# Output projection of a hybrid decoder layer: weight splits in contiguous columns, a strided stationary operand, other last copies and another step order

## The chip, the cores and the metric

One core of a Trainium2 chip runs the whole layer. The metric is the device time of one execution in microseconds (us), as the median of several runs. Five engines work side by side, each with its own instruction list, in order: TensorE (PE; PEld is its weight loading), VectorE (DVE), ScalarE (ACT), GpSimd (POOL) and SyncE (SP), which here issues nearly all transfers. An instruction waits on semaphores that other engines or transfers raise.

## The reference

One decoder layer over 256 tokens of width 1024, all in fp32. What matters here is the end of the token mixer and the beginning of the mixture of experts:

```python
merged = jax.nn.sigmoid(gate_a) * (o_attn @ w_branch_attn[l]) + jax.nn.sigmoid(gate_r) * (o_rwkv @ w_branch_rwkv[l])
h = h + gt1 * (merged @ w_out[l])
xn2 = _rmsnorm(h, moe_norm_g[l]) * (1.0 + sc2) + sh2
moe = _hier_moe(xn2.reshape(B * S, D), ...)
h = h + gt2 * moe.reshape(B, S, D)
```

Before it stand a sparse attention branch (8 heads, with an indexer that selects 64 keys for each query) and an RWKV-7 branch (8 heads, a recurrent state). The experts are 32 SwiGLU MLPs of 1024 x 512; every token uses two of them, and the weights of all 32 are read, 201 MB in all.

## The kernel before, in words

The program has three stretches.

*The mixing stage.* Five generators (rwkv, selection, attention, gate, modulation) yield after each piece of TensorE work, and a loop takes their steps in the order that the string `ORDER` writes out by hand, one letter for a step. `LORD` is the order in which the weights of this stage are loaded. `pump()` issues loads into a large SBUF arena as long as there is room; `RESERVE[stage]` is the room that it leaves free in each stage. All loads go through SyncE's queue, in order, and a load waits until the buffer that it fills has been let go.

*Split matmuls.* [...] `split()` (lines 510 to 521) makes of a weight tile of 512 columns a high part (a copy that rounds to fp32r, by ScalarE, line 519, or GpSimd, line 517) and a low part (weight less high part, line 520, by VectorE or GpSimd). `SPLIT[stage]` says which engines do it, with two letters for each of four splits in turn: "AP" is a copy on ScalarE and a subtraction on GpSimd. `mm3()` (lines 528 to 532) does three matmuls: high x high, high x low, low x high. Split tiles lie in a ring of four pairs of 512 columns.

*The output projection* (lines 1493 to 1514). The merged branches, transposed to channels x tokens, lie in `mh` and `ml` (high and low), 8 blocks of 128 channels. `w_out` comes in four loads of two k each (k is a block of 128 of the 1024 input channels). The 1024 output channels are dealt out to 8 blocks m with a stride of eight: block m holds the channels m, m + 8, m + 16 and so on. Before the change the split reads the weights with that stride, so that the split tile holds four blocks of 128 neighbouring columns, and one split serves four blocks (12 matmuls). In the last round (j = 3) four splits are made and the blocks are finished one by one: residual and gate (line 1506), squares for the norm (lines 1509 to 1513), router logits (line 1471). Then come the routing on VectorE (lines 1549 to 1599), the transposes of h (line 1483) and the first matmuls of the experts.

*The experts.* Quadruples of experts: gather, gate and up projections (lines 1611, 1626, 1632), down projections (line 1653, in the last quadruple 1660 and 1666), merge by a matmul (line 1708). Their weights flow through the arena; a buffer is let go when its matmuls are done, and then SyncE loads the next. At the end `leave()` (lines 1784 to 1793) copies the sums from PSUM, for the second half of the tokens in two parts of 256 columns, and sends them out.

Other lines that are named later: 406 (modulation), 1063 (transposes of x, whose columns are taken eight apart), 1086 and 1101 (selection scores), 360 (a step of a reciprocal root on VectorE), 798 (scores of the rwkv branch), 1172 (transposes of normalised heads), 1323 and 1325 (merging and splitting the branches' sum).

Of the kernel before, what the change touches and what calls it, by code (L numbers as in the profile page):

```python
# [45 lines left out]
INV = 18.0  # L46
SOFT = 4.5
TMAJ = 0.3
NP2 = 4
NPO = 4  # L50
REST = 12.0
SMALL = 2432
WRS = True
MODS = ((0, 0, 0), (1, 0, 0, 1), (1, 0, 0, 1), (1, 0, 0, 0))
ALIGN = 1024
RESERVE = (29696, 12288, 15360, 4096, 0)
FORCE = False
FORCE0 = True
WIDE = 'a'
_S = ("AD", "PD", "AP", "PD")  # L60
SPLIT = (('PD', 'PD', 'AP', 'AD'), ('PD', 'PD', 'AP', 'PD'), ('PP', 'PP', 'AD', 'AD'), ('AD', 'AP', 'AD', 'AD'), ('AD', 'PD', 'AP', 'PD'))
PRIO = ('mod', 'sel', 'rwkv', 'attn', 'gate')
ORDER = 'rrrrrrmrrmmrrmrrmrrrrrrmrrrmmmrrmrmmmmrsrmaarmrmarrramrmamrrmraarrmmaarmarmaasrmmasaasmmsrarssrasraaarrarrarraasrssasssararasgrssssgraargrsrgsrsgggsrrsmgmmgsmrrrrggrgrgrrggggrsaggrrrggrgrrrgagagaggggaaaagggggaaaggaagggagagggaggaaaaagaggaaaaaggaaaaaaaggaggggggggggg'
LORD = (0, 1, 2, 3, 4, 5, 6, 7, 8, 9, 10, 12, 13, 15, 11, 14, 17, 16, 18, 23, 19, 20, 21, 22, 24, 28, 25, 27, 26, 29, 30, 31, 32, 33, 34, 35, 36, 37, 38, 44, 40, 39, 41, 42, 51, 45, 43, 47, 48, 52, 50, 46, 49)
INFO = []
QUADS = NE // 4
ENDS = ((0, 512), (512, 512))
# [90 lines left out]
def layer_kernel(tc, I, out, dbg=None):  # L158
    nc = tc.nc
    dbg = dbg or (lambda name, ap: None)  # L160
    ALL = CFG[2]
    TOT = ALL - 6144 - 1024 * NP2
    RING = CFG[0] * 4096
    ctxs = []

# [8 lines left out]
    NB = {"r": 3, "a": 3, "g": 2, "e": 4}  # L174
    A = Arena(sb.tile([128, TOT], F32, name="arena"), TOT)

    nB2 = 2048 + 1024 * (NP2 - NPO)
    nB = ALL - TOT - nB2
    fr = tc.tile_pool(name="fr", bufs=1)
    B = Arena(fr.__enter__().tile([128, nB], F32R, name="split"), nB)  # L180
    fr2 = tc.tile_pool(name="fr2", bufs=1, side="right")
    B2 = Arena(fr2.__enter__().tile([128, nB2], F32R, name="split2"), nB2)
    state = {"t": 0.0, "dma": 3.0, "next": 0, "stage": 0, "tag": "a", "more": []}

    def MM(lo, hi, shape, dtype=None):
        ap = A.get(*shape, lo=lo, hi=hi, dtype=dtype)
        assert ap is not None, ("arena full", shape)
        return ap

    def M(*shape, dtype=None):  # L190
        small = np.prod(shape) < 300
        ap = A.get(*shape, lo=TOT - SMALL, hi=TOT, dtype=dtype) if small else None
        return MM(RING, TOT if small else TOT - SMALL, shape, dtype) if ap is None else ap

# [12 lines left out]
    def add_ada(r, js):  # L207
        for j in js:
            add_load(("ada", r, j), (1, 2048), [(None, ada[:, j:j + 1, 2048 * r:2048 * r + 2048])])
# [41 lines left out]
    for i, l in enumerate(base):  # L251
        loads.append(l)
        for key in ad[ADAL[i - 14][0]:ADAL[i - 14][1]] if 0 <= i - 14 < len(ADAL) else ():
            add_ada(key[1], (key[2],))
    if LORD:
        loads[:] = [loads[i] for i in LORD]
    INFO.append(len(loads))
# [6 lines left out]
    for q in range(QUADS):  # L264
        for n, name, r in (("eg", "expert_w_gate", 4), ("eu", "expert_w_up", 4), ("ed", "expert_w_down", 2)):
            for i, (c, m) in enumerate(ENDS if n == "ed" and q == QUADS - 1 else ((0, None), (0, None))):
                for e in range(4 * q, 4 * q + 4 if q or n != "eg" or i else 0):
                    w = I[name][0, e].rearrange("(p k) n -> p k n", p=128)
# [7 lines left out]
    def pump():  # L276
        while state["next"] < len(loads):
            key, shape, parts = loads[state["next"]]
            t = A.get(*shape, lo=0, hi=RING, from_top=False)
            if t is None and A.room(RING, TOT - SMALL) >= int(np.prod(shape)) + (RESERVE[state["stage"]] if state["next"] >= nst else 6144):  # L280
                t = A.get(*shape, lo=RING, hi=TOT if state["stage"] == 4 else TOT - SMALL)
            for m in state["more"] if t is None else ():
# [10 lines left out]
    def need(key):  # L293
        assert key in W, ("not loaded", key, list(W))
        return W[key]

    def done(key, then=None):
        t = W.pop(key)
        next(a for a in [A] + state["more"] if id(t) in a.live).free(t)
        if then is not None:  # L300
            then()
        pump()
# [195 lines left out]
    def step(it, keep):  # L498

        return after_last(lambda: next(it, "end"), keep)  # L500
# [4 lines left out]


    cnt_split = [0]
    pairs = [(b.get(512), b.get(512)) for b in [B] * NPO + [B2] * (NP2 - NPO)]

    def split(w, p=None):  # L510

        i = cnt_split[0]
        cnt_split[0] += 1
        h, l = (t.rearrange("p (k n) -> p k n", k=w.shape[1]) for t in pairs[i % len(pairs)])
        p = p or SPLIT[state["stage"]][i % 4]
        if p[0] == "P":
            nc.gpsimd.tensor_scalar(h, w, 1.0, 0.0, op0=OP.mult, op1=OP.add)  # L517
        else:
            nc.scalar.copy(h, w)  # L519
        (nc.gpsimd if p[1] == "P" else nc.vector).tensor_sub(l, w, h.bitcast(F32))  # L520
        return h, l
# [6 lines left out]
    def mm3(ps, l, r, start, stop):  # L528

        nc.tensor.matmul(ps, l[0], r[0], start=start, stop=False)  # L530
        nc.tensor.matmul(ps, l[0], r[1], start=False, stop=False)  # L531
        nc.tensor.matmul(ps, l[1], r[0], start=False, stop=stop)  # L532
# [794 lines left out]
    mh, ml = xhi, xlo  # L1327
# [91 lines left out]
    while todo:  # L1419

        at = {n: max(ready[n], came[blocked[n]] + 0.5) if blocked[n] else ready[n] for n in todo
              if blocked[n] is None or blocked[n] in W}
        want = [n for n in at if nth < len(ORDER) and n[0] == ORDER[nth]]
        if want:
            at = {n: at[n] for n in want}
        t = max(state["t"], min(at.values()))
# [12 lines left out]
        c = step(it, FORCE)  # L1439
# [12 lines left out]
            blocked[n] = c  # L1452
    row2, sh2, s2c, rb, gt1 = (res[n] for n in ("row2", "sh2", "s2c", "rb", "gt1"))
    state["stage"] = 4
    del pairs[NPO:]
    fr2.__exit__(None, None, None)
    state["more"].append(Arena(pool(name="sb1", bufs=1, side="right").tile([128, nB2], F32, name="more0"), nB2))
    A.free(*[c[0] for c in cur.values() if c[0] is not state["nwt"]])
# [9 lines left out]
    def logits(m):  # L1468

        for a in range(2):  # L1470
            nc.tensor.matmul(psl[:, 64 * a:64 * a + 36], h[:, m, 128 * a:128 * a + 128], wrt[:, m, :],  # L1471
                             start=False, stop=False)
# [13 lines left out]
    def block(m):  # L1486
        return pso[m // 2][:, 256 * (m % 2):256 * (m % 2) + 256] if m < 6 else pso[m - 3][:, 0:256]

    def out_part(m, k, w, i):
        mm3(block(m), (w[0][:, i, :], w[1][:, i, :]), (mh[:, k, :], ml[:, k, :]), k == 0 and m > 5,  # L1490
            k == 7 and m not in (0, 2, 4))

    for j in range(4):
        w = need(("wo", j))
        ws = {}
        for hh, kk in ((0, 0), (0, 1), (1, 0), (1, 1)) if j == 3 else ((0, 0), (1, 0), (0, 1), (1, 1)):
            ws[hh, kk] = split(w[:, kk, :].rearrange("p (c k) -> p k c", k=8)[:, 4 * hh:4 * hh + 4, :])
            for i in range(4 if j < 3 else 0):
                out_part(4 * hh + i, 2 * j + kk, ws[hh, kk], i)
            for m in range(4 * hh, 4 * hh + 4 if j == 3 and kk else 0):  # L1500
                for k2 in range(2):
                    out_part(m, 6 + k2, ws[hh, k2], m % 4)
                for n in {3: (0,), 4: (1,), 5: (2,), 6: (3,), 7: (4, 5)}.get(m, ()):
                    logits(n)
                for n in () if m in (0, 2, 4) else (m - 1, m) if m < 6 else (m,):
                    nc.vector.scalar_tensor_tensor(h[:, n, :], block(n), gt1[:, n:n + 1], h[:, n, :], op0=OP.mult, op1=OP.add)
                    sq = hsq[:, 0 if n == 0 else 1 + (n + 1) % 2, :]
                    if n == 7:
                        nc.vector.tensor_mul(sq, h[:, n, :], h[:, n, :])
                    else:  # L1510
                        nc.scalar.activation(sq, h[:, n, :], AF.Square)
                    if 0 < n < 6:
                        nc.gpsimd.tensor_add(hsq[:, 0, :], hsq[:, 0, :], sq)
        done(("wo", j))
# [15 lines left out]
    def ME(*shape, dtype=None):  # L1530
        return next(ap for ap in (a.get(*shape, dtype=dtype) for a in [A] + state["more"]) if ap is not None)
# [144 lines left out]
    acc = [acp.tile([128, 512], F32, name=f"acc{i}") for i in range(4)]  # L1676
# [33 lines left out]
    y = None  # L1710
# [63 lines left out]
    y = ME(2, D)  # L1774
# [9 lines left out]
    def leave(c):  # L1784

        for a in range(2):
            o = acc[2 * a + c // 512]
            if a == 0:
                nc.scalar.copy(y[:, a, c:c + 512], o)
            else:  # L1790
                nc.vector.tensor_copy(y[:, a, c:c + 256], o[:, 0:256])
                nc.scalar.copy(y[:, a, c + 256:c + 512], o[:, 256:512])
            (nc.scalar if a else nc.sync).dma_start(out=out[0, 128 * a:128 * a + 128, c:c + 512], in_=y[:, a, c:c + 512])

    last[0] = None
# [2 lines left out]
    times_gate(0, ps)  # L1798
    after_last(lambda: finish(st, 0, stop=True))
    leave(0)  # L1800
    ps, p4 = PS(), PS()
    after_last(lambda: cols_down(ps, [need(("ed", e, 1)) for e in es[0:3]]))
# [3 lines left out]
    after_last(lambda: finish(st, 512, 96))  # L1806
    after_last(lambda: finish(sl, 512, 128, 0, True))
    leave(512)
    for i in range(2):
        for e in es:  # L1810
# [142 lines left out]
```

## Time and profile before

| | us |
|---|---|
| three runs | 797.19, 797.26, 798.94 |
| median | 797.26 |
| profiled execution | 798.72 |
| its span, first to last instruction | 796.8 |
| TensorE matmuls busy | 676.4 |
| VectorE, ScalarE, GpSimd busy | 285.3, 167.6, 144.2 |
| granted TensorE clock, mean (1 is full) | 0.948 |
| moved by DMA | 261.38 MB, mean 328 GB/s |

The profiled execution lies 1.46 us above the median. Its time holds 1.9 us more than the span. Busy shares are averages over stages of different kinds: in the mixing stage all four compute engines work, in the experts only TensorE and the DMA engines do much. A row of the timeline gives start, duration, engine, line, operation and shapes, and in brackets how long the engine had been idle before and what ended that.

### The profile page before, as it was taken

What the parts mean: (1) busy time and instruction counts of PE and PEld (TensorE: products, weight loads), DVE (VectorE), ACT (ScalarE), POOL (GpSimd) and SP (SyncE); (2) the same over time, 40 slices, a digit from 0 to 9 for tenths busy, and PEclk for the clock granted to TensorE, in tenths of its full rate; (3) what the DMA queues carried; (4) which work ended last, traced back from release to release, by engine and by line L of the source; (5) the groups of instructions that cost most, each with busy time, mean ns of one, the idle gap of its engine ahead of it and who ended that gap; (6) DMA issues with size and microseconds to landing.
All of it is one profiled execution on the core that took longest, in us unless ns stands there. A gap on an engine that the chain in (4) does not pass through costs nothing.

```text
span 796.8 us, 11470 instructions
## 1 busy us (share of the span) xinstructions
PE 676.4 (85%) x4657; PEld 364.7 (46%) x4657; DVE 285.3 (36%) x665; ACT 167.6 (21%) x347; POOL 144.2 (18%) x176
## 2 busy tenths in 40 slices
PE   5897989799998998889999778878768868878667
PEld 2785657468888877853342312312312312312112
DVE  2577789697336557741210160100100100100001
ACT  2445412144156644321110100100100100000000
POOL 1446744331314117610000000000000000000000
PEclk9899999899999999989999899899999999899889
DMA  9997467443656456779999999999999999999994
GB/s 333 389 308 253 165 221 282 146 154 105 218 208 239 133 178 246 292 257 420 422 421 422 421 420 422 421 420 423 420 421 422 420 421 422 420 421 422 422 392 180
DMA packets 63590, 261.38 MB, mean 328 GB/s; under 512 B 7952, under 2 KB 19216, under 8 KB 38448
## 3 DMA queue, kind: packets, MB, share of 16 engines
q1 hardware_dynamic: 63248, 260.11, 83.4%
q8 instruction: 37, 0.61, 0.3%
q10 hardware_dynamic: 288, 0.52, 0.2%
q14 instruction: 17, 0.14, 0.0%
HBM read 259.57 MB, written 1.05 MB: 327 GB/s over the span
## 4 chain that ended last, share of the span: by engine, by line
DMA 46%; PE 10%; DVE 3%; SPq 1%; issue 1%; POOL 1%; ACT 0%; POOLq 0%; DVEq 0%
DMA arena<-in_expert_w_down_dram 17%; DMA arena<-in_expert_w_gate_dram 13%; DMA arena<-in_expert_w_up_dram 12%; DMA more<-in_expert_w_gate_dram 2%; DMA more<-in_expert_w_up_dram 2%; PE ps_e L1626 2%; DVE split L520 1%; PE ps_e L1611 1%; SPq L288 1%; PE ps_e L1660 1%; PE acc L1701 1%; PE acc L1708 1%; PE ps_e L1653 1%; PE ps_e L1632 0%; PE ps_r L1471 0%
## 5 line engine op out<-in xcount | busy, mean ns | idle before, releaser
L1626 PE MATMUL ps_e<-arena,more 128*32 128x512 f32 x440 | 87.6, 656 | 23.9 <-DMA arena<-in_expert_w_gate_dram 12.0
L1626 PE MATMUL ps_e<-arena 128*32 128x512 f32 x416 | 82.4, 682 | 20.4 <-DMA arena<-in_expert_w_gate_dram 11.7
L1653 PE MATMUL ps_e<-arena 128*32 128x512 f32 x360 | 84.3, 609 | 13.5 <-DMA arena<-in_expert_w_down_dram 9.6
L520 DVE TENSOR_TENSOR split<-arena,split 128x512 fp32r<-128x512 f32 x77 | 70.7, 928 | 45.6 <-ACT split L519 31.8
L1637 ACT ACTIVATE arena<-ps_e 128x512 f32<-128x512 f32 x8 | 4.8, 597 | 244.8 <-PE ps_e L1626 244.8
L1638 DVE SCALAR_TENSOR_TENSOR arena<-arena,ps_e 128x512 f32<-128x512 f32 x8 | 5.5, 688 | 140.2 <-ACT arena L1637 140.2
L1691 POOL TENSOR_TENSOR arena<-arena 128x256 f32<-128x256 f32 x8 | 4.9, 615 | 280.7 <-PE ps_e L1694 279.0
L1670 DVE TENSOR_TENSOR arena<-ps_e,more 128x512 f32<-128x512 f32 (+1 forms) x17 | 11.8, 691 | 122.2 <-PE ps_e L1653 109.1
L519 ACT CAST split<-arena 128x512 fp32r<-128x512 f32 x66 | 45.0, 688 | 48.1 <-PE ps_g L531 30.3
L520 POOL TENSOR_TENSOR split<-arena,split 128x512 fp32r<-128x512 f32 x33 | 47.2, 1431 | 42.6 <-ACT split L519 27.8
L564 PE MATMUL ps_a<-split 128*128 128x256 f32 x360 | 52.1, 304 | 3.1 <-ACT split L476 1.9
L1626 PEld LDWEIGHTS ps_e<-arena,more 128*32 128x32 f32 x440 | 19.4, 118 | 76.3 <-issue 30.9
L564 PEld LDWEIGHTS ps_a<-split 128*128 128x128 f32 x360 | 47.9, 205 | 12.1 <-issue 6.5
L1626 PEld LDWEIGHTS ps_e<-arena 128*32 128x32 f32 x416 | 17.8, 122 | 74.0 <-issue 35.8
L517 POOL TENSOR_SCALAR split<-arena 128x512 fp32r<-128x512 f32 x44 | 36.9, 842 | 70.2 <-PE ps_g L531 18.7
L1653 PEld LDWEIGHTS ps_e<-arena 128*32 128x32 f32 x360 | 19.6, 110 | 64.3 <-issue 31.2
L530 PE MATMUL ps_g<-split 128*128 128x256 f32 x128 | 39.1, 306 | 0.0
L532 PE MATMUL ps_g<-split 128*128 128x256 f32 x128 | 36.9, 289 | 2.0 <-POOL split L520 2.0
L1639 DVE SCALAR_TENSOR_TENSOR arena<-arena,ps_e 128x512 f32<-128x512 f32 x8 | 8.2, 1029 | 82.5 <-PE ps_e L1626 82.5
L531 PE MATMUL ps_g<-split 128*128 128x256 f32 x128 | 36.8, 288 | 0.0
L1611 PEld LDWEIGHTS ps_e<-arena,more 128*128 128x128 f32 x256 | 30.7, 195 | 13.2 <-issue 8.2
L532 PE MATMUL ps_a<-split 128*128 128x256 f32 (+1 forms) x96 | 30.4, 317 | 6.2 <-DVE split L520 6.2
(378 smaller groups left out, 1192.5 us busy)
## 6 DMA issues: line engine op xcount, KB each, us to landing
arena<-in_expert_w_gate_dram SPq DMA_DIRECT2D x54, 1024.0 KB, 19.8
arena<-in_expert_w_up_dram SPq DMA_DIRECT2D x53, 1024.0 KB, 19.8
arena<-in_expert_w_down_dram SPq DMA_DIRECT2D x53, 1024.0 KB, 19.8
arena<-in_w_in_dram SPq DMA_DIRECT2D x18, 1024.0 KB, 7.8
arena<-in_ada_w_dram SPq DMA_DIRECT2D x16, 1024.0 KB, 6.1
more<-in_expert_w_up_dram SPq DMA_DIRECT2D x11, 1024.0 KB, 19.8
more<-in_expert_w_down_dram SPq DMA_DIRECT2D x11, 1024.0 KB, 19.8
arena<-in_ada_w_dram SPq DMA_DIRECT2D x16, 512.0 KB, 10.9
```

Source lines behind the costliest of these rows:

```text
L517: nc.gpsimd.tensor_scalar(h, w, 1.0, 0.0, op0=OP.mult, op1=OP.add)
L519: nc.scalar.copy(h, w)
L520: (nc.gpsimd if p[1] == "P" else nc.vector).tensor_sub(l, w, h.bitcast(F32))
L530: nc.tensor.matmul(ps, l[0], r[0], start=start, stop=False)
L531: nc.tensor.matmul(ps, l[0], r[1], start=False, stop=False)
L532: nc.tensor.matmul(ps, l[1], r[0], start=False, stop=stop)
L564: nc.tensor.matmul(p, a[:, kk, :], b[:, 4 * hf + kk, :], start=(i == 0 and kk == KORD[0]), stop=(i == 2 and kk == KORD[-1]))
L1611: nc.tensor.matmul(ps[:, n * kk:n * kk + n], h2[:, a, 2 * k2 + kk, :], oh(a), start=(a == 0), stop=(a == 1))
L1626: nc.tensor.matmul(ps[32 * g:32 * g + 32, :], xg[:, 4 * i + k, 32 * g:32 * g + 32], w[:, k, :], start=(i == 0 and k == 0), stop=(i == 1 an ...
L1639: nc.vector.scalar_tensor_tensor(hidb[0:r].rearrange("p (j q) -> p q j", j=4), thb[0:r].rearrange("p (q j) -> p q j", j=4), 0.5, psu[0:r, ...
L1653: nc.tensor.matmul(pss[c][32 * g:32 * g + 32, :], hTb[:, 2 * i + j, 32 * g:32 * g + 32], w[:, j, 512 * c:512 * c + 512], start=(i == 0 and ...
L1670: nc.vector.tensor_mul(Yb[0:r, c:c + 512], ps[0:r], gt2[0][0:r, g:g + 512])
```

## The change

Four things are done.

1. In the output projection the weights are split as they lie, in two halves of 512 neighbouring columns for each k. The four ring pairs are now two wide pairs of 1024 columns, cut in halves. The matmuls take block m as every eighth column of the wide tile: the stride of eight is now in TensorE's stationary operand. A matmul needs both halves. The order of the loops is k, then m over all eight blocks; in the last round k = 6 and k = 7 are both split first, and then the blocks are done one by one with both. The count of splits is made even first (it is 94 in both kernels before the projection).
2. `leave()`: for each half of the tokens one copy of 512 columns, the first by ScalarE, the second by VectorE.
3. `ORDER`, `LORD` and `RESERVE` (stages 1 and 2 leave more room free), and the fourth split in turn of stage 1 is copied by ScalarE in place of GpSimd.
4. `NP2` and `NPO` go, with the same sizes of all pools.

```diff
-RESERVE = (29696, 12288, 15360, 4096, 0)
+RESERVE = (29696, 17408, 24576, 4096, 0)
...
-SPLIT = (('PD', 'PD', 'AP', 'AD'), ('PD', 'PD', 'AP', 'PD'), ('PP', 'PP', 'AD', 'AD'), ('AD', 'AP', 'AD', 'AD'), ('AD', 'PD', 'AP', 'PD'))
+SPLIT = (('PD', 'PD', 'AP', 'AD'), ('PD', 'PD', 'AP', 'AD'), ('PP', 'PP', 'AD', 'AD'), ('AD', 'AP', 'AD', 'AD'), ('AD', 'PD', 'AP', 'PD'))
...
-    pairs = [(b.get(512), b.get(512)) for b in [B] * NPO + [B2] * (NP2 - NPO)]
+    wide = [(B.get(1024), B.get(1024)) for _ in range(2)]
+    pairs = [tuple(t[:, 512 * i:512 * i + 512] for t in p) for p in wide for i in range(2)]
...
-    def out_part(m, k, w, i):
-        mm3(block(m), (w[0][:, i, :], w[1][:, i, :]), (mh[:, k, :], ml[:, k, :]), k == 0 and m > 5,
+    def out_part(m, k, w):
+        mm3(block(m), (w[0][:, m:1024:8], w[1][:, m:1024:8]), (mh[:, k, :], ml[:, k, :]), k == 0 and m > 5,
             k == 7 and m not in (0, 2, 4))
 
+    cnt_split[0] += cnt_split[0] % 2
     for j in range(4):
         w = need(("wo", j))
-        ws = {}
-        for hh, kk in ((0, 0), (0, 1), (1, 0), (1, 1)) if j == 3 else ((0, 0), (1, 0), (0, 1), (1, 1)):
-            ws[hh, kk] = split(w[:, kk, :].rearrange("p (c k) -> p k c", k=8)[:, 4 * hh:4 * hh + 4, :])
-            for i in range(4 if j < 3 else 0):
-                out_part(4 * hh + i, 2 * j + kk, ws[hh, kk], i)
-            for m in range(4 * hh, 4 * hh + 4 if j == 3 and kk else 0):
+        ws = []
+        for kk in range(2):
+            ws.append(wide[cnt_split[0] // 2 % 2])
+            for hh in range(2):
+                split(w[:, kk:kk + 1, 512 * hh:512 * hh + 512])
+            if j < 3:
+                for m in range(8):
+                    out_part(m, 2 * j + kk, ws[kk])
+                continue
+            for m in range(8 if kk else 0):
                 for k2 in range(2):
-                    out_part(m, 6 + k2, ws[hh, k2], m % 4)
+                    out_part(m, 6 + k2, ws[k2])
...
         for a in range(2):
-            o = acc[2 * a + c // 512]
-            if a == 0:
-                nc.scalar.copy(y[:, a, c:c + 512], o)
-            else:
-                nc.vector.tensor_copy(y[:, a, c:c + 256], o[:, 0:256])
-                nc.scalar.copy(y[:, a, c + 256:c + 512], o[:, 256:512])
+            (nc.vector.tensor_copy if a else nc.scalar.copy)(y[:, a, c:c + 512], acc[2 * a + c // 512])
```

The strings `ORDER` and `LORD` say little by themselves; two places show what moves. (Line numbers of the changed kernel are one or two lower here: its 529 to 531 are 530 to 532 before, 404 is 406, 1085 is 1086, 1100 is 1101, 516 is 517, 519 is 520, 1322 is 1323.)

TensorE in the mixing stage, around the first matmuls of the selection, before. `ps_a`, `ps_r`, `ps_g` are PSUM tiles of attention and selection, of rwkv, and of gates and modulation; the rows of 128x512 are the query projection, six to a weight chunk:

```order
L532 MATMUL ps_a<-split 128x512
L1086 MATMUL ps_a<-arena 128x8 x2
L809 MATMUL ps_r<-arena 128x128 x4
L406 MATMUL ps_g<-arena 32x512
L1101 MATMUL ps_a<-arena 128x128 x2
L406 MATMUL ps_g<-arena 32x512 x3
L530 MATMUL ps_a<-split 128x512
```

and in the changed kernel:

```order
L531 MATMUL ps_a<-split 128x512
L808 MATMUL ps_r<-arena 128x128 x4
L529 MATMUL ps_a<-split 128x512
L1085 MATMUL ps_a<-arena 128x8 x2
L530 MATMUL ps_a<-split 128x512
L531 MATMUL ps_a<-split 128x512
L529 MATMUL ps_a<-split 128x512
L404 MATMUL ps_g<-arena 32x512 x4
L1100 MATMUL ps_a<-arena 128x128 x2
L530 MATMUL ps_a<-split 128x512
```

The rwkv transposes and four matmuls of the next weight chunk, and all of line 406, now stand ahead of the first matmuls of line 1101.

GpSimd in the output projection, before (517 is a copy, 520 a subtraction, 1323 a sum of the branches):

```order
L520 TENSOR_TENSOR split<-arena,split 128x512
L517 TENSOR_SCALAR split<-arena 128x512
L1323 TENSOR_TENSOR arena<-arena 128x512
L517 TENSOR_SCALAR split<-arena 128x512
L520 TENSOR_TENSOR split<-arena,split 128x512
L517 TENSOR_SCALAR split<-arena 128x512 x2
```

and in the changed kernel:

```order
L519 TENSOR_TENSOR split<-arena,split 128x512
L516 TENSOR_SCALAR split<-arena 128x512
L1322 TENSOR_TENSOR arena<-arena 128x512
L516 TENSOR_SCALAR split<-arena 128x512 x2
L519 TENSOR_TENSOR split<-arena,split 128x512
L516 TENSOR_SCALAR split<-arena 128x512 x2
```

From the second even k on, GpSimd now copies its half of that k before it subtracts the other half, which ScalarE copies.

## Rows read from the trace of the kernel before

**Rows 1.** The page, bandwidth in 40 slices of the span.
```profile
GB/s 333 389 308 253 165 221 282 146 154 105 218 208 239 133 178 246 292 257 420 422 421 422 421 420 422 421 420 423 420 421 422 420 421 422 420 421 422 422 392 180
```

**Rows 2.** The chain of waits in order of time: start, us, what.
```profile
387.77 16.59 DMA more<-in_expert_w_up_dram
...
776.18 5.14 PE ps_e L1660 x26
...
792.73 0.37 ACT arena L1792
```

**Rows 3.** Windows around the output projection: busy us by engine, clock, DMA share, GB/s.
```profile
320.00:330.00 10.00, 9.24 (x75) 9.04 (x76) 7.92 (x6) 3.41 (x4) 7.76 (x4) 1.00 0.96 398
330.00:340.00 10.00, 8.46 (x69) 7.87 (x67) 6.66 (x10) 3.17 (x7) 5.02 (x7) 1.00 0.65 222
340.00:350.00 10.00, 7.22 (x56) 6.11 (x56) 6.17 (x47) 4.36 (x16) 1.49 (x3) 0.79 0.52 160
...
360.00:370.00 10.00, 10.00 (x94) 3.82 (x94) 1.86 (x5) 1.41 (x3) 0.00 (x0) 1.00 1.00 419
```

**Rows 4.** Timeline of TensorE in the output projection.
```profile
307.63 0.28 PE L530 MATMUL ps_a<-split 128*128 128x256 f32 x1
...
309.18 0.28 PE L531 MATMUL ps_a<-split 128*128 128x256 f32 x1
...
333.51 0.38 PE L532 MATMUL ps_a<-split 128*128 128x256 f32 x1 [1.43 <-DVE split L520]
...
336.03 0.64 PE L1471 MATMUL ps_r<-arena 128*128 128x36 f32 x4
336.49 0.36 PE L530 MATMUL ps_a<-split 128*128 128x256 f32 x1
...
340.65 0.28 PE L532 MATMUL ps_r<-split 128*128 128x256 f32 x1
```

**Rows 5.** Split tiles, forms: min/median/max ns; first 0 to 245 us, then 308 to 335.
```profile
L520 DVE TENSOR_TENSOR split<-arena,split x47: 675/691/2520, 21.3 to 244.9; 128x512 fp32r<-128x512 f32 x47
L517 POOL TENSOR_SCALAR split<-arena x36: 610/618/1657, 19.0 to 226.3; 128x512 fp32r<-128x512 f32 x36
L519 ACT CAST split<-arena x33: 601/618/666, 21.9 to 243.2; 128x512 fp32r<-128x512 f32 x33
L520 POOL TENSOR_TENSOR split<-arena,split x22: 1252/1278/1872, 20.3 to 244.3; 128x512 fp32r<-128x512 f32 x22
...
L520 DVE TENSOR_TENSOR split<-arena,split x12: 1098/1600/2428, 308.9 to 334.5; 128x512 fp32r<-128x512 f32 x12
L519 ACT CAST split<-arena x6: 1122/1178/1201, 310.6 to 329.6; 128x512 fp32r<-128x512 f32 x6
```

**Rows 6.** Timeline of GpSimd, the first subtraction of the output projection.
```profile
305.55 1.66 POOL L520 TENSOR_TENSOR split<-arena,split 128x512 fp32r<-128x512 f32 x1
```

**Rows 7.** Weight loads of transposes, lines 1063 and 1172; then three loads in the timeline.
```profile
L1063 PEld LDWEIGHTS ps_r<-arena x16: 188/192/208, 234.7 to 240.1; 128*128 128x128 f32 x16
...
L1172 PEld LDWEIGHTS ps_a<-arena x16: 137/140/143, 180.7 to 190.7; 128*128 128x128 f32 x16
...
235.15 0.41 PEld L1063 LDWEIGHTS ps_r<-arena 128*128 128x128 f32 x3 [0.24 <-issue]
```

**Rows 8.** Timeline of TensorE and VectorE around line 1086; TensorE's waits before 308 us.
```profile
142.12 0.28 PE L1086 MATMUL ps_a<-arena 8*128 8x8 f32 x2 [2.35 <-DVE arena L360]
...
145.90 0.68 PE L1101 MATMUL ps_a<-arena 32*128 32x128 f32 x4 [1.93 <-DVE arena L365]
146.51 1.06 PE L406 MATMUL ps_g<-arena 128*32 128x512 f32 x6
...
136.89 0.68 DVE L520 TENSOR_TENSOR split<-arena,split 128x512 fp32r<-128x512 f32 x1
...
PE ps_r L798 <- DVE arena L761: 3.0, 1, 3.0
```

**Rows 9.** Last copies, line 1791, forms: min/median/max ns.
```profile
L1791 DVE COPY arena<-acc x2: 424/424/424, 784.1 to 792.3; 128x256 f32<-128x256 f32 x2
```

More of the change, by code (lines that the diff above doesn't have):

```diff
@@ L48 @@
 TMAJ = 0.3
-NP2 = 4
-NPO = 4
 REST = 12.0
@@ L60 @@
 _S = ("AD", "PD", "AP", "PD")
-SPLIT = (('PD', 'PD', 'AP', 'AD'), ('PD', 'PD', 'AP', 'PD'), ('PP', 'PP', 'AD', 'AD'), ('AD', 'AP', 'AD', 'AD'), ('AD', 'PD', 'AP', 'PD'))
+SPLIT = (('PD', 'PD', 'AP', 'AD'), ('PD', 'PD', 'AP', 'AD'), ('PP', 'PP', 'AD', 'AD'), ('AD', 'AP', 'AD', 'AD'), ('AD', 'PD', 'AP', 'PD'))
 PRIO = ('mod', 'sel', 'rwkv', 'attn', 'gate')
-ORDER = 'rrrrrrmrrmmrrmrrmrrrrrrmrrrmmmrrmrmmmmrsrmaarmrmarrramrmamrrmraarrmmaarmarmaasrmmasaasmmsrarssrasraaarrarrarraasrssasssararasgrssssgraargrsrgsrsgggsrrsmgmmgsmrrrrggrgrgrrggggrsaggrrrggrgrrrgagagaggggaaaagggggaaaggaagggagagggaggaaaaagaggaaaaaggaaaaaaaggaggggggggggg'
-LORD = (0, 1, 2, 3, 4, 5, 6, 7, 8, 9, 10, 12, 13, 15, 11, 14, 17, 16, 18, 23, 19, 20, 21, 22, 24, 28, 25, 27, 26, 29, 30, 31, 32, 33, 34, 35, 36, 37, 38, 44, 40, 39, 41, 42, 51, 45, 43, 47, 48, 52, 50, 46, 49)
+ORDER = 'mrrrrrrrrmmrmrrmrrrrrmrrrarmmrmrrmmmmrrrmarmmrmarrramrmamrrsraarmmraarmarmmaasrmmsaaaasmmsrarssrarrsaraarrararrsaasrsasssagrarssssgsraargrsrgsrsgggsrrmgmmgsmrrrrggrgrsgrrggggrsaggrrrggaggrgrrrgagagaggagaaggggaaaggaaggggaggagaggaaaagaaggaaaaaggaaaaaaggagagggggggggg'
+LORD = (0, 1, 2, 3, 4, 5, 6, 7, 8, 9, 10, 13, 15, 11, 12, 14, 17, 16, 18, 23, 19, 20, 21, 22, 24, 28, 25, 27, 29, 26, 30, 31, 32, 33, 34, 35, 36, 37, 38, 44, 39, 40, 41, 51, 45, 49, 42, 48, 43, 47, 52, 46, 50)
 INFO = []
@@ L161, in layer_kernel @@
     ALL = CFG[2]
-    TOT = ALL - 6144 - 1024 * NP2
+    TOT = ALL - 10240
     RING = CFG[0] * 4096
@@ L175, in layer_kernel @@
     A = Arena(sb.tile([128, TOT], F32, name="arena"), TOT)
-    nB2 = 2048 + 1024 * (NP2 - NPO)
+    nB2 = 2048
     nB = ALL - TOT - nB2
@@ L1454, in layer_kernel @@
     state["stage"] = 4
-    del pairs[NPO:]
     fr2.__exit__(None, None, None)
```

## Prediction

> **What bounds the kernel now.** I read first the page's bandwidth row. From the nineteenth slice on it stands at 420 to 423 GB/s [rows 1], and before that it is well below: the second half of the program is a stream of expert weights that runs as fast as it ever does. The reader is to see where that plateau begins. The chain of waits says what sets its end [rows 2]: at 387.77 us it passes from TensorE's work to transfers, and then it is transfer after transfer until 776.18, when the last matmuls of the experts, the merge and the copies out take the remaining 20 us.
>
> So the end is the start of the saturated stream plus a fixed number of bytes. The windows show that start [rows 3]: DMA share 0.52 from 340 to 350 us, 1.00 from 360. The stream cannot start earlier, because the buffers that it fills are freed by work that comes behind the output projection. I conclude that whatever makes that projection end earlier moves the plateau and the end by about as much, as long as the DMA engines keep room ahead of the plateau. They do: a share of 0.65 where the projection runs out, from 330 to 340 us, and of 0.52 behind it.
>
> Then the projection itself, in TensorE's timeline [rows 4]. Its first matmul starts at 307.63 us, its last at 340.65: 33.0 us. Undisturbed, matmuls follow each other by (309.18 - 307.63) / 13 = 0.119 us. There are 8 blocks x 8 k x 3 = 192, so 191 x 0.119 = 22.8 us of them; four insertions of router logits (336.03, next matmul at 336.49) cost some 0.5 us each, 2.0 us. The rest, 33.0 - 22.8 - 2.0 = **8.2 us, is stall**. A row with a bracket names the cause: TensorE waits for line 520 on VectorE, the low half of a split weight tile (333.51, one of six such rows).
>
> Why are the splits late? Compare the same operation on the same shape in two stretches [rows 5]. In the projection the input is read with a stride of eight elements, elsewhere it is contiguous: ScalarE's copy takes 1.18 us against 0.62, VectorE's subtraction 1.60 against 0.69, at best 1.10.
>
> **The change part by part.** *Splits read contiguously, 16 of them.* I take the contiguous medians: copy 0.62 on either engine, VectorE's subtraction 0.69, GpSimd's 1.28. In the new order every k needs two halves before its 24 matmuls (24 x 0.119 = 2.86 us). For even k (copy on ScalarE and on GpSimd side by side, then the subtractions, GpSimd's behind its own copy) the slower arm is 0.62 + 1.28 = 1.90 us. For odd k both subtractions are VectorE's: 0.62 + 2 x 0.69 = 2.00 us. There are two wide buffers, so the split of k + 2 starts when k's matmuls end and has the 2.86 us of k + 1 as cover: k = 1 to 6 cost nothing. If that cover is gone (subtractions at the 1.10 of a disturbed VectorE), an odd k takes 2.82 us and still just fits.
>
> Two places are not covered. For k = 0 GpSimd comes to its subtraction at 305.55 as now (it has other work until then) [rows 6]: 305.55 + 1.28 + 0.62 (the other half's copy) + 0.69 = 308.14, where the third matmul wants it at 307.63 + 2 x 0.119 = 307.87: 0.3 us. And the last round has changed: k = 6 and 7 are used together, block by block, and the buffer of k = 7 is free only when k = 5 has ended. TensorE does five matmuls (0.6 us), then waits until 2.00: 1.4 us. [...] The new stall is 2.5 us, **the saving 8.2 - 2.5 = 5.7 us**. Bounds: 8.2 if nothing stalls, 2.9 if VectorE's subtractions take 1.3 us (odd k 3.2 us, four times 0.4 over the cover, and 1.2 more at k = 7).
>
> *The stride of eight moves to TensorE's stationary operand, 192 loads.* The trace has that read once: line 1063 transposes x with its columns eight apart, as stationary operand [rows 7]. Its loads take 192 ns where the contiguous transposes of line 1172 take 140, so the stride is not free in latency. But three of them in a row take 0.41 us, so they follow each other by (0.41 - 0.19) / 2 = 0.11 us. That is below the matmuls' 0.119, and loads run beside matmuls. I count nothing, and keep the upper end for a rival: these were transposes of fp32, not loads of fp32r.
>
> [...]
>
> *The step order.* TensorE's list changes over the mixing stage; the place that the trace prices is the one shown at line 1086 [rows 8]. There TensorE waited 2.35 us for VectorE (line 360, inside a chain that the change does not shorten) and 1.93 us more at line 1101. The second weight chunk of the query projection was split at 136.89 + 0.68 and lay idle behind these waits. Now four matmuls of it, of 512 columns each, and the last three of line 406 run before the second wait: 4 x 2 x 0.119 = 0.95 us, and the 1.06 us of line 406, 2.0 us of work that no longer comes after. Lower bound: one new wait like that of line 798, -3.0 us; upper bound: both waits gone, 4.3 us. [...] The larger reserves and the new load order shift loads on SyncE's queue by a few places, the last gate weights behind branch and output weights; no wait of TensorE before 308 us names a gate, branch or output weight, so I count nothing, and the lower bound covers it.
>
> *Last copies.* On the path now: VectorE 0.42 us, then ScalarE 0.37, the second waiting for the first [rows 9, 2]: 792.28 to 793.10. After: one copy of 512 on VectorE, which by its 0.69 for the same width with two operands [rows 5] ends at 792.97. **0.1 us**. At most 0.3 either way.
>
> **Sum.** 5.7 + 1.5 + 0.1 = 7.3 us. The profiled execution took 798.72 us, which is 1.46 over the median of the three runs shown, 797.26; it would become 791.4, and the median 790.0. Its own range is 784.7 (8.2 and 4.3) to 794.5 (2.9 and no gain from the order). A measurement of this kernel can tell about 0.3%, 2.4 us, from no change.
>
> **The rivals.**
> *A, slower: TensorE's loads become the bound.* If the stationary read pays per element what ScalarE's pays, (1.18 - 0.62) / 512 = 1.09 ns, a load of 128 columns takes 0.14 us more, its pitch is 0.25 and 192 x (0.25 - 0.119) = 25 us are added, with all 8.2 us of stall now hidden: 797.3 + 25 - 8.2 - 1.6 = 812.5 us. It decides from a pitch of 0.119 + 9.8 / 192 = 0.170 on. For it: the 52 ns of latency. Against: the pitch of 0.11. Chance 0.12.
> *B, nothing gained: the splits were slow from sharing, not from stride.* Line 520's spread from 1.10 to 2.43 us in the projection says that GpSimd and VectorE hinder each other too. Subtractions of 1.3 us save 2.9 us, and a new wait of a microsecond or so in the changed order takes part of it back: 795.4 us. Against: ScalarE, which shows no such spread, is slowed nearly twofold as well. Chance 0.13.
> *C, the change does nothing that lasts: the stream does not move.* From 320 to 330 us the DMA share is 0.96 [rows 3]; if the transfers there bound what comes later, an earlier end of the projection only lengthens the wait behind it: 797.2 us. Against: 0.65 and 0.52 in the next two windows. Chance 0.05.
>
> **How the numbers follow.** The forecast has 0.70: 790.0 us. The range reaches from its lower end, 784.5, to 797.3, taking in B and C and leaving out A, 0.12, and a little beyond either end. Faster by over 0.3% is below 794.9: nearly all of the forecast and a third of B, 0.74. Slower is A and a little of a lost order, 0.13. The rest, 0.13, lies within 0.3%.
>
> **What would show it.** In the new profile: splits of the projection at 0.62 and 0.69 us; its matmuls 0.12 us apart, strided loads longer than contiguous ones but not further apart; one wait of 1 to 2 us ahead of the last 48 matmuls and no other above half a microsecond; first to last matmul about 27 us; first routing matmul and the DMA plateau 6 to 7 us earlier; the waits at lines 1086 and 1101 shorter or filled. I am wrong if the matmuls come 0.17 us apart or more, if VectorE's subtractions stay above 1.1 us, if the projection starts later than now, or if the plateau does not move with its end.

## The result and the profile after

The changed kernel takes 810.03 us (median of four runs, 808.81 to 811.51) against 798.1 us before. The ratio is 1.0151, with a 95% interval of 1.0133 to 1.0168: it is **slower by 1.5%**. One execution among those below, of the projection with the old tables, took 1936.58 us and is left out of that kernel's figures. The prediction said 790.0 us, with 784.5 to 797.3 as its range. What came is its rival A, priced there at 812.5 us and given a chance of 0.12.

The profiled execution took 811.51 us, span 809.7 us, 12.9 us more than the span before. The first place to look is where the stream of expert weights becomes saturated, since the prediction took the end to be that point plus fixed bytes. The page's bandwidth row [rows 1] after the change:

```profile
GB/s 336 391 307 227 165 277 197 180 185 98 225 211 250 123 260 294 105 89 387 423 420 422 421 421 422 420 422 421 420 422 423 420 422 421 420 423 421 421 396 206
```

The plateau is as high as before, and in the two slices ahead of it (a slice is 20 us) the rate has fallen from 292 and 257 to 105 and 89 GB/s. The chain of waits [rows 2] now passes to transfers at 401.70 us, before at 387.77, and from there it is nearly all transfers in both (7.5 us of TensorE's work came between at 505.31 before, 4.5 us of TensorE's and VectorE's at 778.22 now). Its first transfer and its last row, the new last copy:

```profile
401.70 17.08 DMA more<-in_expert_w_up_dram
...
805.26 0.69 DVE arena L1790
```

The windows around the projection [rows 3] (busy us and count of TensorE, its loads, VectorE, ScalarE, GpSimd; granted clock; DMA share; GB/s):

```profile
310.00:320.00 10.00, 10.00 (x44) 10.00 (x43) 2.16 (x3) 0.89 (x2) 1.21 (x3) 1.00 0.96 370
320.00:330.00 10.00, 10.00 (x43) 10.00 (x43) 1.99 (x3) 0.98 (x2) 2.76 (x3) 1.00 0.25 76
330.00:340.00 10.00, 10.00 (x43) 10.00 (x43) 1.99 (x3) 1.25 (x2) 3.02 (x3) 1.00 0.17 69
340.00:350.00 10.00, 10.00 (x50) 10.00 (x50) 3.11 (x7) 2.87 (x7) 3.64 (x5) 0.88 0.32 105
350.00:360.00 10.00, 9.96 (x47) 9.03 (x46) 2.94 (x20) 2.23 (x6) 0.00 (x0) 0.50 0.31 105
```

The columns to read are the first two. Up to 350 us TensorE is never idle, and neither are its loads; yet from 320 to 340 us it gets through 43 matmuls in 10 us, where it did 75 and 69 with stalls in it before. The split engines have little to do. The projection has gone from waiting for splits to being bound by its own loads. TensorE's timeline [rows 4] gives the pace:

```profile
302.05 0.51 PE L529 MATMUL ps_a<-split 128*128 128x256 f32 x1
...
303.12 0.41 PE L529 MATMUL ps_a<-split 128*128 128x256 f32 x1
...
322.38 0.40 PE L531 MATMUL ps_a<-split 128*128 128x256 f32 x1
...
350.36 0.45 PE L530 MATMUL ps_r<-split 128*128 128x256 f32 x1
350.61 0.45 PE L531 MATMUL ps_r<-split 128*128 128x256 f32 x1
```

From 303.12 to 322.38 there are 80 matmuls: **0.241 us each, where it was 0.119**. First to last is 350.61 - 302.05 = 48.6 us, before 33.0. The forms of the split tiles (min/median/max ns) [rows 5, 7]:

```profile
L530 PEld LDWEIGHTS ps_a<-split x48: 312/337/341, 302.3 to 346.2; 128*128 128x128 f32 x48
...
L519 DVE TENSOR_TENSOR split<-arena,split x12: 676/692/1765, 302.0 to 338.3; 128x512 fp32r<-128x512 f32 x12
L516 POOL TENSOR_SCALAR split<-arena x8: 619/624/1060, 300.9 to 337.1; 128x512 fp32r<-128x512 f32 x8
L518 ACT CAST split<-arena x7: 620/622/625, 300.4 to 337.0; 128x512 fp32r<-128x512 f32 x7
```

The splits are as fast as forecast, 0.62 and 0.69 us. The stride of eight has moved to a reader that has 192 reads to do in a row.

So in this execution: the projection starts 307.63 - 302.05 = 5.6 us earlier, lasts 15.6 us longer, ends 10.0 us later. Line 1704, which puts h into the experts' sums and is the first large work behind the routing (1701 before), starts at 362.91 instead of 349.53, 13.4 us later, and the end is 12.9 us later. Of the 3.4 us that come in behind the projection, more below.

### The profile page after: what moved, and what is told of

It reads as the page before. It is cut to its first block, busy times and chain, and to the rows that moved or that the text cites. A ratio compares the mean times of both kernels' runs of the same rounds, so it can differ in the third digit from the quotient of the medians.

```text
span 809.7 us, 11463 instructions
## 1 busy us (share of the span) xinstructions
PE 695.5 (86%) x4657; PEld 389.3 (48%) x4657; DVE 276.4 (34%) x665; ACT 165.2 (20%) x350; POOL 132.7 (16%) x171
## 4 chain that ended last, share of the span: by engine, by line
DMA 48%; PE 14%; DVE 1%; POOL 1%; ACT 0%; issue 0%; SPq 0%; POOLq 0%
DMA arena<-in_expert_w_down_dram 14%; DMA arena<-in_expert_w_gate_dram 12%; DMA arena<-in_expert_w_up_dram 12%; DMA more<-in_expert_w_up_dram 5%; DMA more<-in_expert_w_down_dram 3%; DMA more<-in_expert_w_gate_dram 2%; PE ps_e L1629 2%; PE ps_a L531 1%; PE ps_a L529 1%; PE ps_a L530 1%; PE ps_e L1614 1%; PE acc L1704 1%; PE ps_e L1656 1%; PE ps_r L1469 1%; PE ps_r L529 0%; PE ps_r L530 0%
## 5 line engine op out<-in xcount | busy, mean ns | idle before, releaser
L1629 PE MATMUL ps_e<-arena,more 128*32 128x512 f32 x440 | 87.4, 662 | 25.3 <-DMA arena<-in_expert_w_gate_dram 12.8
L1656 PE MATMUL ps_e<-arena 128*32 128x512 f32 x360 | 83.7, 599 | 15.0 <-DMA arena<-in_expert_w_down_dram 11.1
L1629 PE MATMUL ps_e<-arena 128*32 128x512 f32 x416 | 79.2, 638 | 19.2 <-DMA arena<-in_expert_w_gate_dram 11.0
L519 DVE TENSOR_TENSOR split<-arena,split 128x512 fp32r<-128x512 f32 x77 | 61.1, 802 | 58.3 <-POOL split L516 30.1
L518 ACT CAST split<-arena 128x512 fp32r<-128x512 f32 x71 | 43.3, 618 | 74.0 <-PE ps_g L530 29.4
L519 POOL TENSOR_TENSOR split<-arena,split 128x512 fp32r<-128x512 f32 x33 | 45.5, 1377 | 51.3 <-ACT split L518 28.2
L516 POOL TENSOR_SCALAR split<-arena 128x512 fp32r<-128x512 f32 x39 | 26.4, 678 | 83.5 <-PE ps_r L530 20.2
L529 PE MATMUL ps_g<-split 128*128 128x256 f32 x128 | 38.3, 299 | 0.0
L1614 PEld LDWEIGHTS ps_e<-arena,more 128*128 128x128 f32 x256 | 30.9, 196 | 12.9 <-issue 8.2
L529 PE MATMUL ps_a<-split 128*128 128x256 f32 (+1 forms) x96 | 36.8, 383 | 0.1
L531 PE MATMUL ps_g<-split 128*128 128x256 f32 x128 | 36.3, 284 | 0.3 <-POOL split L519 0.3
L530 PE MATMUL ps_a<-split 128*128 128x256 f32 (+1 forms) x96 | 36.2, 377 | 0.0
```

The lines of the kernel that those rows point to most:

```text
L1614: nc.tensor.matmul(ps[:, n * kk:n * kk + n], h2[:, a, 2 * k2 + kk, :], oh(a), start=(a == 0), stop=(a == 1))
L1629: nc.tensor.matmul(ps[32 * g:32 * g + 32, :], xg[:, 4 * i + k, 32 * g:32 * g + 32], w[:, k, :], start=(i == 0 and k == 0), stop=(i == 1 an ...
L1656: nc.tensor.matmul(pss[c][32 * g:32 * g + 32, :], hTb[:, 2 * i + j, 32 * g:32 * g + 32], w[:, j, 512 * c:512 * c + 512], start=(i == 0 and ...
```

## The experiments

Each ratio is to runs of the kernel before on the same chip; its median there was 796.79 us beside the first four experiments and 797.65 beside the others (797.23, a single execution, beside the second probe of transposes).

**The stride alone.** The stationary operand is read from adjacent columns:

```
-  (w[0][:, m:1024:8], w[1][:, m:1024:8])
+  (w[0][:, 128 * m:128 * m + 128], w[1][:, 128 * m:128 * m + 128])
```

> The changed kernel with one thing undone: TensorE reads 128 adjacent columns of the split tile instead of every eighth one, so the 24 matmuls of a k compute other channels than the reference's; counts, sizes, buffers, splits and step order stay. Theory S (the stride on the stationary operand is the whole loss): the projection's matmuls come 0.119 us apart instead of 0.241, its 192 matmuls lose 192 x 0.122 = 23 us, of which some 2 us come back as waits for splits; it starts at 302 us, ends near 329 instead of 350.6, and the time is 786 to 789 us. Rival W (the wide tiles in fp32r or the splits beside them slow the loads, not the stride): the pitch stays above 0.2 us, 805 to 810 us.

Measured: 783.73 us, ratio to before 0.9835 (0.9808 to 0.9861). First and last matmul in TensorE's timeline, and the loads' form:

```profile
299.73 0.28 PE L529 MATMUL ps_a<-split 128*128 128x256 f32 x1
...
325.76 0.28 PE L531 MATMUL ps_r<-split 128*128 128x256 f32 x1
```

```profile
L530 PEld LDWEIGHTS ps_a<-split x48: 188/192/192, 299.7 to 323.2; 128*128 128x128 f32 x48
```

Theory S holds, a little better than its numbers: 26.0 us first to last instead of 48.6, with loads of 192 ns. With buffers, splits and order untouched, rival W is out. One thing besides the stride does differ: a block of adjacent columns lies in one half of the tile, so its matmuls wait for one split and not for both. In the last round the second half's subtraction ran from 319.14 to 319.83 us, while matmuls ran on from 318.36 without a stall. The ratios of the two kernels to before differ by 0.032, some 25 us; 192 x (0.241 - 0.119) = 23.4 us is what the loads account for.

**The parts apart.** First the tables alone (step order, load order, reserves, split table) on the kernel before:

```
-RESERVE = (29696, 12288, 15360, 4096, 0)
+RESERVE = (29696, 17408, 24576, 4096, 0)
...
-ORDER = 'rrrrrrmrrmmrrmrrmrrrrrr...
+ORDER = 'mrrrrrrrrmmrmrrmrrrrrmr...
```

> The kernel before with the new step order, load order, reserves and split table alone; projection and last copies as before. Theory S (the order brought the projection forward by 5.6 us, 307.63 to 302.05, and the projection then lost it): the projection starts near 302 us, lasts 33 us, and the time is 791.5 to 794 us. Rival P (the order is worth the 1.5 us of the prediction, and the rest of the earlier start comes from the projection's own first splits): 796 to 797 us.

Then the reverse, the changed kernel with the four old tables:

> The changed kernel with the step order, load order, reserves and split table of the kernel before: the projection and the last copies alone. Theory S: the projection starts near 307.6 us, lasts 48.6 us, ends near 356, and the time is 813 to 817 us. Rival P (the earlier start belongs to the projection's own splits): it starts near 304, 809 to 811 us.

Measured: the tables alone 792.91 us, ratio 0.9934 (0.9910 to 0.9959); the projection and last copies alone 812.03 us, ratio 1.0199 (1.0162 to 1.0236). Their first and last matmuls of the projection, the tables alone first:

```profile
302.13 0.28 PE L530 MATMUL ps_a<-split 128*128 128x256 f32 x1
...
335.13 0.28 PE L532 MATMUL ps_r<-split 128*128 128x256 f32 x1
```

```profile
306.63 0.47 PE L529 MATMUL ps_a<-split 128*128 128x256 f32 x1
...
354.72 0.40 PE L531 MATMUL ps_r<-split 128*128 128x256 f32 x1
```

The earlier start belongs to the tables, 302.13 us with the old projection; that projection lasts the same 33.0 us in its new place. By how much, a single profile tells only roughly: with the new tables the projection starts between 298.76 and 302.13 us in nine profiles, with the old ones at 306.63 and 307.63 in two. The order is worth 3.9 us by the medians (796.79 to 792.91) and 5.3 us by the ratio, whose interval is 3.3 to 7.2 us, and so much better than forecast. The waits of TensorE from 95 to 305 us (total, times, longest), the kernel before first, then the tables alone, show that it is not where the prediction looked:

```profile
PE ps_a L1086 <- DVE arena L360: 2.4, 1, 2.4
PE ps_g L532 <- POOL split L520: 2.0, 1, 2.0
PE ps_a L1101 <- DVE arena L365: 1.9, 1, 1.9
```

```profile
PE ps_a L1086 <- DVE arena L360: 2.0, 1, 2.0
PE ps_a L1101 <- DVE arena L367: 1.7, 1, 1.7
...
PE ps_g L532 <- POOL split L520: 0.3, 1, 0.3
```

The waits at lines 1086 and 1101, from which 1.5 us were forecast, shrank by 0.4 and 0.2 us. The largest that went is one the prediction did not name, for GpSimd's subtraction in a split ahead of line 532, 2.0 to 0.3 us. All waits listed for this stretch add up to 12.5 us before and 10.1 with the new tables, 2.4 us of the 5.5 by which the start came earlier. What the order gave beyond these waits was not taken apart.

**A layout that spares both readers.** If the price is paid per run of neighbours, a tile in pairs of channels should cost neither side: the split takes two adjacent columns out of every eight and writes them adjacent, TensorE reads every second column. This is the kernel before with the new tables and

```
-  split(w[:, kk, :].rearrange("p (c k) -> p k c", k=8)[:, 4 * hh:4 * hh + 4, :])
+  split(w[:, kk, :].rearrange("p (c j i) -> p j c i", j=4, i=2)[:, 2 * hh:2 * hh + 2])
...
-  (w[0][:, i, :], w[1][:, i, :])
+  (w[0][:, i // 2, :, i % 2], w[1][:, i // 2, :, i % 2])
```

> The kernel before with the new step order, and the split tile laid out in pairs of channels: the split reads two adjacent columns out of every eight and writes them adjacent, TensorE reads every second column as stationary operand. If two adjacent elements are enough for both readers (theory S with a price per run of elements): splits at 0.62 and 0.69 us, matmuls 0.119 us apart, 786 to 790 us. If any stride on the stationary operand costs as the stride of eight does (rival): pitch 0.24 us, 808 to 811 us. If the splits stay at 1.2 to 1.6 us and the pitch at 0.119: as with the order alone, 791.5 to 794 us.

Measured: **783.95 us, ratio 0.9844 (0.9814 to 0.9875)**, 1.6% faster than before, with the whole layer computed. Of the 12.8 us between the medians 3.9 come with the tables alone, so the layout is worth 9.0 us (792.91 to 783.95). Its loads and splits, then its first and last matmul:

```profile
L532 PEld LDWEIGHTS ps_a<-split x48: 195/195/201, 298.8 to 322.5; 128*128 128x128 f32 x48
...
L521 DVE TENSOR_TENSOR split<-arena,split x12: 677/694/1796, 299.1 to 318.5; 128x512 fp32r<-128x512 f32 x12
L518 POOL TENSOR_SCALAR split<-arena x8: 682/896/1164, 297.9 to 317.8; 128x512 fp32r<-128x512 f32 x8
L520 ACT CAST split<-arena x7: 681/708/736, 297.4 to 316.3; 128x512 fp32r<-128x512 f32 x7
```

```profile
298.76 0.28 PE L531 MATMUL ps_a<-split 128*128 128x256 f32 x1
...
325.11 0.28 PE L533 MATMUL ps_r<-split 128*128 128x256 f32 x1
```

The load takes 195 ns at a stride of two against 192 for adjacent columns; VectorE's subtraction is back at 0.69 us, ScalarE's copy at 0.71 instead of 1.18 (0.62 for adjacent columns), GpSimd's copy at 0.90 instead of 1.62 (0.84 in the run with adjacent columns, at the same pace of matmuls). The projection lasts 26.4 us. This is what the change was after, nearly without its price.

**How far apart is too far.** The changed kernel with a stride of four on the stationary operand:

```
-  w[0][:, m:1024:8]
+  w[0][:, 512 * (m // 4) + m % 4:512 * (m // 4) + 512:4]
```

If four costs what eight did, loads take 337 ns, matmuls come 0.241 us apart and the projection lasts 48 us. Rival G has less:

> The changed kernel with the stationary operand read at a stride of four elements of 4 bytes instead of eight, in two halves of the tile, so that other channels are computed than the reference's; all else as in the changed kernel. [...] Rival G (the price grows with the distance): a pitch between 0.13 and 0.22 us, projection 28 to 44 us.

One execution, 804.7 us. First and last matmul, and the loads:

```profile
300.16 0.40 PE L529 MATMUL ps_a<-split 128*128 128x256 f32 x1
...
346.55 0.39 PE L531 MATMUL ps_r<-split 128*128 128x256 f32 x1
```

```profile
L530 PEld LDWEIGHTS ps_a<-split x48: 329/329/333, 300.3 to 342.5; 128*128 128x128 f32 x48
```

329 ns and 46.4 us: nearly all of the price of eight (337 ns, 48.6 us), and rival G, with 28 to 44 us, is out. The step lies between a stride of two elements, where loads took 195 ns, and one of four. Why it lies there is not shown. The splits, which ran near their full pace with two neighbours of every eight columns (ScalarE's copy 0.71 us, 0.62 for adjacent columns) and at about half of it with one (1.18), were not tried at a stride of four.

**Why line 1063 misled.** The prediction took the pace of strided loads from transposes. Six groups of eight operations behind the projection of the changed kernel:

> The changed kernel with 48 operations on TensorE added behind the projection, results unused: eight each of matmuls of the fp32r tile with its columns eight apart and adjacent, of transposes of the same tile read as fp32 eight apart and adjacent, and of plain fp32 matmuls eight apart and adjacent, all with 128 moving columns (fp32r: 128 of the activations). Theory M (what is loaded for a transpose or a plain fp32 matmul is paced in another way than for an fp32r matmul): strided transposes stay near 0.11 us apart, strided fp32r matmuls 0.24 us. Rival B (the three and four transposes of line 1063 were too few, and the first ones hid the pace): eight strided transposes in a row come 0.24 us apart too.

One execution; the other two groups ran while the clock changed. Loads in TensorE's timeline (start, us for all of the row): fp32r eight apart, strided transposes, plain fp32 eight apart, plain fp32 adjacent:

```profile
349.56 1.99 PEld L1523 LDWEIGHTS ps_g<-split 128*128 128x128 f32 x8
...
352.89 1.57 PEld L1527 LDWEIGHTS ps_g<-arena,split 128*128 128x128 f32 x8
...
355.72 3.89 PEld L1531 LDWEIGHTS ps_g<-arena,split 128*128 128x128 f32 x16
359.51 1.89 PEld L1533 LDWEIGHTS ps_g<-arena,split 128*128 128x128 f32 x16
```

Taking one load's duration off a row and dividing by the loads but one: fp32r 0.236 us (337 ns each), plain fp32 0.237 (336 ns), adjacent 0.113 (192 ns). Type made no difference for these matmuls, against theory M as put here, which set plain fp32 apart from fp32r. The transposes came 0.19 us apart, but the clock had fallen to 0.50 from 352 to 355 us, so that row decides nothing. They were run again, straight behind the projection, with the forms of their loads (min/median/max ns) below the timeline:

> The changed kernel with 16 transposes added straight behind the projection, at the full clock, results unused: eight of the split tile's columns eight apart, then eight of adjacent columns. Theory M (a transpose's load is paced in another way than a matmul's): the eight strided ones come about 0.11 us apart, as the four of line 1063, the adjacent ones 0.06 to 0.09. Rival B (runs of three and four were too short to show the pace): the eight come 0.19 to 0.24 us apart.

```profile
348.38 1.04 PEld L1523 LDWEIGHTS ps_g<-arena,split 128*128 128x128 f32 x8
...
349.33 0.91 PEld L1525 LDWEIGHTS ps_g<-arena,split 128*128 128x128 f32 x8
```

```profile
L1523 PEld LDWEIGHTS ps_g<-arena,split x8: 191/193/254, 348.4 to 349.2; 128*128 128x128 f32 x8
...
L1525 PEld LDWEIGHTS ps_g<-arena,split x8: 139/140/142, 349.3 to 350.1; 128*128 128x128 f32 x8
```

One execution, at the full clock: strided (1.04 - 0.19) / 7 = 0.12 us, adjacent (0.91 - 0.14) / 7 = 0.11 us, the latter slower than theory M had it. In what concerns transposes theory M holds: with the same 128 columns at the same stride, the transposes' loads came at half the spacing of the matmuls', 0.12 us against 0.24. Why is not shown; the traces show only that it is the operation, not the number in a row (eight strided matmuls were as far apart as 192) and not fp32 against fp32r.

**The half clock behind the projection.** The changed kernel once more, unedited:

> The changed kernel once more, unedited. If the half clock that began inside its projection at 347.8 us and lasted to 368 us belongs to the kernel, it is there again and the time is 809 to 811 us; if it was one execution's, the clock falls behind the projection for some 7 us as in the kernel before, and the profiled execution is some 3 us shorter than its fellows.

Measured: 807.98 us, ratio 1.0127 (1.0101 to 1.0153); the profiled execution, 807.35 us, is not the 3 us shorter than its fellows (807.07 to 808.89) that one of the two expectations wanted. Its windows:

```profile
340.00:350.00 10.00, 10.00 (x57) 10.00 (x57) 3.85 (x9) 2.87 (x7) 3.65 (x5) 1.00 0.17 72
350.00:360.00 10.00, 8.00 (x43) 5.51 (x42) 6.09 (x49) 3.87 (x14) 0.85 (x2) 0.62 0.65 213
360.00:370.00 10.00, 10.00 (x66) 5.41 (x65) 1.52 (x6) 0.81 (x2) 0.00 (x0) 0.87 0.95 374
```

The projection again takes 48.1 us (300.60 to 348.71), but now the clock falls after it, for 10 us, and line 1704 follows 9.2 us behind the last matmul (8.9 before the change) instead of 12.3. So the 3.4 us extra in the first profile belong to that execution and not to the kernel: there the half clock (0.50) began in the last of the strided matmuls and held over the routing, whose eight logits matmuls took 1.76 us instead of 0.98. The kernel's own loss is 1.3 to 1.5%.

**Pairs with the last copies of the change.**

```
+  (nc.vector.tensor_copy if a else nc.scalar.copy)(y[:, a, c:c + 512], acc[2 * a + c // 512])
```

> The layout in pairs with the new step order (as e4_pairs) and the last copies of the change: the best of both. Expected 783.5 to 784.5 us, below both kernels; the last copies give 0.1 us, which shows in the tail of the trace alone: one copy of 0.69 us behind the last matmuls where there were 0.43 and 0.37 in turn.

Measured: 785.19 us, ratio 0.9833 (0.9804 to 0.9862), a little above what was expected and not to be told from the 0.9844 without the last copies. The tail of the chain, of the pairs without and with it:

```profile
773.41 3.65 PE acc L1709 x8
777.08 0.43 DVE arena L1792
777.54 0.37 ACT arena L1793
```

```profile
775.46 3.65 PE acc L1709 x8
779.13 0.69 DVE arena L1788
```

0.85 us behind the matmuls become 0.71.

## Why the prediction was wrong, step by step

*What bounds the kernel: right.* The end follows the start of the saturated stream in every run that adds nothing behind the projection: the projection's end came 10.0 us later and line 1704 13.4 us later in the changed kernel, the span 12.9 us; with pairs its end at 325.11 us is 15.5 us earlier, and the span 781.7 is 15.1 us shorter. In the other five kernels and the second profile of the change the two shifts agree within 0.9 us. Rival C falls.

*Splits read contiguously: right.* Forecast 0.62 and 0.69 us, and so they came; forecast a projection of about 27 us, and with the stride taken off the loads it took 26.0 us. The saving was put at 5.7 us, and that run had 7.0 (33.0 - 26.0). Of the 2.5 us of new stall, 0.8 stood for restarts and handoffs beside 0.3 and 1.4, and no run shows them. In the trace before, the matmul behind VectorE's subtraction, which ended at 308.87 + 3.95 = 312.82 us, began at 312.88, and the next one at 313.10, 0.22 us later where 0.119 is the pace: 0.06 and 0.10 us. With adjacent columns all that came beside matmuls and logits was 26.0 - 22.8 - 2.0 = 1.2 us, 0.7 of it a wait for VectorE. The 7.0 us are no clean measure, since that run's matmuls wait for one half each: the stall of 1.4 us ahead of the last 48 matmuls did not come there, and in the changed kernel it is hidden by the slow loads. (The bound of 2.9 us counts four covered odd k, where there are three.) Rival B falls with it. In the run with adjacent columns GpSimd was busy 7.04 us from 300 to 310 us, about as before (7.26 to 7.76), and VectorE's subtraction is down from 1.60 to 0.69 us:

```profile
L519 DVE TENSOR_TENSOR split<-arena,split x12: 676/692/1787, 300.0 to 319.1; 128x512 fp32r<-128x512 f32 x12
```

Its maximum is 1.79 us. In the changed kernel the longest one, 1.76 us at 309.11, ran beside a subtraction of GpSimd's begun at 309.04; another, at 320.39 beside one begun at 320.44, took 0.69. What made the long ones long is not shown.

*"I count nothing" for the stride on the stationary operand: this step failed.* The prediction put the stride on TensorE's loads at 0 us; it was worth +23.4 us of loads, or 48.6 - 26.0 = 22.6 us of projection. The pace of 0.11 us was read correctly, but from transposes, and a matmul's load of the same columns is paced at 0.24 us. The doubt stood in the text (fp32, not fp32r) and had the wrong object: type does not matter, the operation does. The latencies already said little: 192 ns for a strided transpose is also what adjacent fp32r loads take (188 to 192 in the rows here). With a proxy so unlike, ScalarE's nearly doubled copy on the very same columns was the nearer row, and rival A, built on it, gave a pitch of 0.25 us where 0.241 came; loads grew by 145 ns (192 to 337), where its price for 128 elements was 140. Why ScalarE's price per element fits TensorE's loads and not the transposes is not shown. It should have had the larger chance. Its break-even pitch of 0.170 us was also right in kind: at 0.24 all of the old stall is hidden, and the loss shows in full.

*Step order: right in sign, under-sized, for another reason.* 1.5 us forecast, 3.9 to 5.3 measured, near or over the upper bound of 4.3, which was both named waits gone; they hardly changed (by 0.4 and 0.2 us). No run shows that 0.5 of the 2.0 us of moved work is lost again.

*Last copies: right.* 0.1 us forecast, 0.14 us in the tail.

The sum as it was: 22.6 - 7.0 = 15.6 us lost in the projection, less 0.1 for the copies and 3.9 to 5.3 for the order, makes 10.2 to 11.6 us slower, against 10.3 (807.98 - 797.65) and 11.9 us (810.03 - 798.1) measured.

## What to carry to other kernels

Moving a stride from one engine to another is no saving until the new reader's pace is known from an operation of the same kind: read the spacing of loads from matmuls, not from transposes (0.24 against 0.12 us here), and count how many reads in a row there are. Before choosing a side, look for a layout between: here pairs of neighbours let the split (VectorE's subtraction 0.69 us) and the load (195 ns) both run at nearly full pace, for 9.0 us on 793. When a price has two proxies that far apart, let the plain reading of the same bytes by another engine weigh as much as the one on the same engine with another operation.

## What was not expected of the hardware

Under the stride of eight, matmuls were 0.24 to 0.25 us apart at both clocks: 350.36 and 350.61 us in the timeline above lie in the stretch at 0.50 of the full clock, those from 303.12 to 322.38 at 1.00. Their spacing did not follow TensorE's granted clock. Strided transposes, 0.12 us apart at the full clock, were 0.19 apart at the half. And the length of a half-clock stretch varied between executions of the same kernel, from 10 to 20 us behind this projection, which moves a single profile by some 3 us.
